# The mixer gates of a decoder layer as seven block products by tokens, ahead of all branch projections

## The chip, the cores and the metric

The kernel runs on one core of one Trainium2 chip. The metric is the device time of one execution in microseconds (us). Three runs of the kernel before gave 1073.43, 1072.18 and 1070.83 us, so the median is 1072.18 us.

The engines are named as in the profile: PE (TensorE, matrix products), PEld (its weight loads), DVE (VectorE), ACT (ScalarE), POOL (GpSimd) and SP (SyncE, here only a queue that issues transfers). A matmul has a moving operand, 512 or 256 columns wide here, and a stationary operand of 128 x 128, which PEld loads.

## The reference

One layer of a hybrid decoder on x of 512 tokens by 1024 features, in fp32. What matters here:

```python
proj = x @ w_in                       # q, k, v of three mixers, and gates: 3 x 1024 columns
o_da, o_sb, o_dl = ...                # three causal attentions, each 512 tokens x 512 features
g = sigmoid(gates).reshape(B, S, 3, D)
merged = g[0] * (o_da @ w_branch_da) + g[1] * (o_sb @ w_branch_sb) + g[2] * (o_dl @ w_branch_dil)
x = layer_norm(alpha * x + merged @ w_out)                       # LayerNorm 1
c = square(relu(x @ w_up)) @ w_down
ple = sigmoid(x @ w_ple_gate) * (p @ w_ple)
x = layer_norm(alpha * x + c + ple)                              # LayerNorm 2
```

## The kernel before

Precision. Every large fp32 product is made of three products in fp32r. Both factors are split into a high part and a rest, and h·h, h·l and l·h are added up in one PSUM bank. So each block of a product costs three matmuls. Weights arrive in **chunks** of 128 x 1024 fp32 (512 KB). A chunk is loaded by SP into one of 4 raw buffers (`fill`, `raw`, L207). ACT then casts it to the high part (`wh`, L235) and DVE subtracts to get the rest (`wl`, L238). There are 7 buffers for split chunks (`RING`), so splitting runs up to 7 chunks ahead of the matmuls that use them.

Items. The program is a list of **items**. One item is a run of matmuls into one PSUM bank (`mm`) and what takes the result out of it (`ev`). The loop at the end of `trunk` writes the items out one after the other. It issues the evacuation of the item before, splits one or two chunks (`pump`), adds up some weights (`add`), and calls `step`, which moves each attention head that is under way on by one piece. A head is a generator: its logits, its softmax and its value product are separate pieces. An item that yields in the middle of its matmuls gets a second `step` there. From this list a planner makes a fixed order for each engine, normally that of the list, but it places work that is ready ahead of work that it expects to be waiting.

Buffers. PSUM has 8 banks: 2 `mm` banks, which the items use in turn, and 6 `at` banks for the heads, for transposes and for sums that stay open over several items. SBUF has 48 general slots of 128 x 512 fp32 (`slot`) and two buffers of 8 x 512 columns with the tags XH and XL, which hold x transposed (`xhT`, `xlT`) and later LayerNorm 1's output transposed (`x1hT`, `x1lT`).

The order of items. Item 0 and the 58 after it project q, k, v (`t_item`: weights stationary, x moving, the result transposed, 24 matmuls; `v_items`: x stationary, weights moving, the result by tokens, 24 matmuls). Then come the **gates**: 24 `t_item`s, one per gate and 128 columns, each evacuated to a slot `graw`. Six come ahead of the first branch item. The rest alternate with the **branch items** (L401 to L427): for each of 8 column tiles three items of 12 matmuls, then the sigmoid (L394), a multiplication (L416), an addition (L420), and a split of the merged column tile into `mh` and `ml` (L425, L426). The sb and dil heads have to be done before item 65, the da heads before item 70. `wout_items` (L519 to L521) multiply the merged tiles, stationary, by w_out. LayerNorm 1 follows per 128 tokens (`ln1_gen`): four transposes per half (L567), splits into XH and XL (L551, L552). The next product, the input gate of the embedding (`wg_items`), and the MLP are already done by **seven products** of half-sized blocks in place of eight (Strassen's scheme in Winograd's form). It needs sums of weight blocks and of operand blocks.

Weight sums. `totals` queues the sums of weight blocks. Each set of four blocks takes four copies from DRAM to DRAM on SP (L174) and four accumulating transfers on POOL (L176). Each of the latter also waits for a recent cast of ACT, so that they keep pace. `add` issues the next one of the list, from item 24 on in the kernel before.

Of the kernel before, what the change touches and what calls it, by code (L numbers as in the profile page):

```python
# [9 lines left out]
F32 = mybir.dt.float32  # L10
# [7 lines left out]
P = 128  # L18
# [16 lines left out]
def main_order():  # L35
# [14 lines left out]
    for j in range(8):  # L50
        for i in range(3):
            o += [("T", "gate", 8 * i + j)]
# [3 lines left out]
def trunk(tc, a, out):  # L56
    nc = tc.nc
    es = ExitStack()
    with es:
# [209 lines left out]
        gate_raw = {}  # L269
# [16 lines left out]
        def t_evac(name, j):  # L286
            def ev(ps):
# [5 lines left out]
                elif name == "gate":  # L293
                    t = slot("graw")
                    cp(t, ps)
                    gate_raw[j] = t
# [75 lines left out]
        for kind, name, j in order[2:]:  # L372
            if kind == "T":
                if name == "gate":
                    continue
# [10 lines left out]
        sg = {}  # L386

        last_exp = [None]

        def gate_sig(i, j):  # L390
            t = gate_raw.pop(8 * i + j)

            with tc.issue_after(last_exp[0]):
                nc.scalar.activation(t, t, AF.Sigmoid)  # L394
            sg[i, j] = t

        def branch_items(j, between=()):
            c1 = chunk(a["wb1"][j].rearrange("p k m -> p (k m)"), 1024)
            c2 = chunk(a["wb2"][j].rearrange("p k m -> p (k m)"), 512)
            for n, i in enumerate((1, 2, 0)):  # L400
                if n == 2:  # L401
                    for t in between:
                        t_item(*t)
                    if j == 0:
                        first_da.append(len(items))
                def mm(ps, i=i):
                    c = c2 if i == 2 else c1
                    for k in range(4):
                        s = slice(((i % 2) * 4 + k) * P, ((i % 2) * 4 + k) * P + P)
                        h, lo = oTs[4 * i + k]  # L410
                        mm3(ps, c["h"][:, s], c["l"][:, s], h, lo, k == 0, k == 3)

                def ev(ps, i=i, n=n):
                    gate_sig(i, j)
                    g = sg.pop((i, j))
                    nc.vector.tensor_mul(g, g, ps)  # L416
                    if n == 0:
                        merged[j] = g
                    else:
                        nc.vector.tensor_add(merged[j], merged[j], g)  # L420
                    if n == 2:
                        m = merged[j]
                        h = slot("mh", F32R)
                        lo = slot("ml", F32R)
# [1199 lines left out]
```

## Time and profile before

| | |
|---|---|
| median of three runs | 1072.18 us (1070.83 to 1073.43) |
| the profiled execution, its own time | 1073.58 us |
| its span, first to last instruction | 1071.8 us |
| granted PE clock over the span | 0.998 |
| busy: PE, PEld, DVE, ACT, POOL | 1056.0, 907.8, 719.9, 528.3, 83.0 us |
| moved by DMA | 203.87 MB, mean 190 GB/s |

How to read it: a matmul's row has a modelled end, so matmuls overlap in the rows. What counts is the distance from one start to the next. Rows of the view by windows have the stretch, its length, then per engine the busy time and in brackets the number of instructions, then the granted PE clock, the share of time in which the DMA engines were busy, and GB/s. Rows of the view by time have start, duration, engine, line, operation, output<-inputs, shapes and count; in square brackets stands how long the engine had been idle and what ended that. Rows of the view by lines end with busy time, mean duration in ns, and idle time before.

### The profile page before, as it was taken

How to read it: one execution, taken by the hardware profiler on the slowest of the kernel's cores; microseconds unless marked ns; L12 is line 12 of the kernel's file. 1: busy time of each engine (PE TensorE's matmuls, PEld its weight loads, DVE VectorE, ACT ScalarE, POOL GpSimd, SP SyncE). 2: the span in 40 equal slices, each digit the busy share in tenths (PEclk: the TensorE clock that was granted, in tenths of full speed). 3: DMA queues.
4: the chain of work that ended last, by engine and by line, in shares of the span. 5: the costliest groups of instructions: out<-in, count | busy, mean ns of one | idle time of the engine just before them, and what ended most of it. 6: DMA issues, size and time to landing. Idle time of an engine off the chain costs nothing. (4 is left out here: it accounts for less than half of the span.)

```text
span 1071.8 us, 14697 instructions
## 1 busy us (share of the span) xinstructions
PE 1056.0 (99%) x5543; PEld 907.8 (85%) x5543; DVE 719.9 (67%) x1264; ACT 528.3 (49%) x866; POOL 83.0 (8%) x106
## 2 busy tenths in 40 slices
PE   8999999999999999999999999999999999999996
PEld 6888788999888888888888888888989989989985
DVE  5988577656443756655444445898786787787786
ACT  5665445435232545545333333375666567557551
POOL 0000200010011101011101110100100010000000
PEclk9999999999999999999999999999999999999999
DMA  7643545393777647575798757349989895655722
GB/s 275 189 175 123 174 166 134 122 255 98 236 217 199 192 139 209 172 204 163 202 259 226 189 160 243 110 132 279 245 215 258 253 257 194 196 177 178 236 79 79
DMA packets 61624, 203.87 MB, mean 190 GB/s; under 512 B 7387, under 2 KB 8299, under 8 KB 60465
## 3 DMA queue, kind: packets, MB, share of 16 engines
q1 hardware_dynamic: 41536, 164.03, 43.9%
q0 software_dynamic: 19440, 37.98, 20.5%
q8 instruction: 43, 0.70, 0.3%
q10 hardware_dynamic: 576, 0.92, 0.2%
q14 instruction: 29, 0.23, 0.1%
HBM read 200.78 MB, written 73.42 MB: 256 GB/s over the span
## 5 line engine op out<-in xcount | busy, mean ns | idle before, releaser
L235 ACT CAST wh<-raw 128x1024 fp32r<-128x1024 f32 (+1 forms) x231 | 238.9, 1036 | 296.6 <-PE mm L88 159.5
L238 DVE TENSOR_TENSOR wl<-raw,wh 128x1024 fp32r<-128x1024 f32 (+1 forms) x231 | 277.2, 1205 | 141.0 <-ACT wh L235 137.1
L87 PE MATMUL mm<-xhT,wh 128*128 128x512 f32 x496 | 196.4, 396 | 0.0
L89 PE MATMUL mm<-xhT,wl 128*128 128x512 f32 x496 | 194.2, 392 | 0.0
L88 PE MATMUL mm<-xlT,wh 128*128 128x512 f32 x496 | 194.0, 391 | 0.0
L89 PEld LDWEIGHTS mm<-xhT,wl 128*128 128x128 f32 x496 | 93.2, 188 | 19.6
L87 PEld LDWEIGHTS mm<-xhT,wh 128*128 128x128 f32 x496 | 93.3, 188 | 19.3 <-issue 1.1
L88 PEld LDWEIGHTS mm<-xlT,wh 128*128 128x128 f32 x496 | 93.3, 188 | 17.9
L744 PE MATMUL mm<-x1hT,wh 128*128 128x256 f32 x256 | 72.5, 283 | 2.4 <-DVE cut L756 2.4
L746 PE MATMUL mm<-x1hT,wl 128*128 128x256 f32 x256 | 72.5, 283 | 0.0
L745 PE MATMUL mm<-x1lT,wh 128*128 128x256 f32 x256 | 72.5, 283 | 0.0
L348 PE MATMUL mm<-wh,xhT 128*128 128x512 f32 x160 | 64.8, 405 | 0.0
L350 PE MATMUL mm<-wh,xlT 128*128 128x512 f32 x160 | 63.2, 395 | 0.0
L349 PE MATMUL mm<-wl,xhT 128*128 128x512 f32 x160 | 63.0, 394 | 0.0
L744 PE MATMUL mm<-xs,wh 128*128 128x256 f32 x192 | 54.5, 284 | 0.0
L745 PE MATMUL mm<-xs,wh 128*128 128x256 f32 x192 | 54.4, 283 | 0.0
L746 PE MATMUL mm<-xs,wl 128*128 128x256 f32 x192 | 54.3, 283 | 0.0
L176 POOL DMA_DIRECT2D total<-total x34 | 30.2, 954 | 278.7 <-ACT wh L235 233.1
L744 PEld LDWEIGHTS mm<-x1hT,wh 128*128 128x128 f32 x256 | 49.1, 192 | 2.8 <-issue 2.6
L745 PEld LDWEIGHTS mm<-x1lT,wh 128*128 128x128 f32 x256 | 49.1, 192 | 0.3
L746 PEld LDWEIGHTS mm<-x1hT,wl 128*128 128x128 f32 x256 | 49.2, 192 | 0.0
L350 PEld LDWEIGHTS mm<-wh,xlT 128*128 128x128 f32 x160 | 37.9, 237 | 3.9
(388 smaller groups left out, 2187.1 us busy)
## 6 DMA issues: line engine op xcount, KB each, us to landing
raw<-total SPq DMA_DIRECT2D x68, 512.0 KB, 4.3
raw<-in_wt_dram SPq DMA_DIRECT2D x62, 512.0 KB, 4.8
total<-total POOLq DMA_DIRECT2D x34, 512.0 KB, 9.5
total<-in_wu_dram SPq DMA_DIRECT2D x32, 512.0 KB, 6.8
total<-in_wd_dram SPq DMA_DIRECT2D x28, 512.0 KB, 6.6
raw<-in_wd_dram SPq DMA_DIRECT2D x25, 512.0 KB, 4.5
raw<-in_wu_dram SPq DMA_DIRECT2D x24, 512.0 KB, 4.6
raw<-in_wv_dram SPq DMA_DIRECT2D x20, 512.0 KB, 4.5
```

Of the source, the lines that this page charges most:

```text
L87: nc.tensor.matmul(ps, wh, xh, start=start, stop=False, skip_group_check=True)
L88: nc.tensor.matmul(ps, wh, xl, start=False, stop=False, skip_group_check=True)
L89: nc.tensor.matmul(ps, wl, xh, start=False, stop=stop, skip_group_check=True)
L176: i = nc.gpsimd.dma_start(t, s, accum_op=OP.add, max_dma_last_dim=2048)
L235: i = nc.vector.tensor_copy(h, raw) if c.get("dve") else nc.scalar.copy(h, raw)
L238: i = nc.vector.tensor_sub(lo, raw, h.bitcast(F32))
L348: nc.tensor.matmul(ps, x1, c["h"][:, s], start=k == 0, stop=False)
L349: nc.tensor.matmul(ps, x1, c["l"][:, s], start=False, stop=False)
L350: nc.tensor.matmul(ps, x2, c["h"][:, s], start=False, stop=k == 7)
L744: nc.tensor.matmul(o, c["h"][:, s], h, start=first, stop=False, skip_group_check=True)
L745: nc.tensor.matmul(o, c["h"][:, s], lo, start=False, stop=False, skip_group_check=True)
L746: nc.tensor.matmul(o, c["l"][:, s], h, start=False, stop=last, skip_group_check=True)
```

## The change

The gates leave `t_item`. For each of the three gates (in the order 1, 2, 0) `seven` makes 14 items of 12 matmuls: seven products of a 256-token block of x by a 512 x 512 block of weights, each for two tiles of 128 tokens. x is stationary now, the weights move, and the result is by tokens. All 42 stand ahead of all branch items (items 59 to 100). Six more sets of weight sums are queued, ahead of all others, and `add` begins at item 7 with other rates. The operand sums of x are made from x loaded again (`x_load`, `x_sum`).

The branch items become 8 per branch by tokens: oT is stationary, the weights move. Branch 0 (da) is first, then 2, then 1, the last by rows. Heads of sb and dil leave oT whole, and `halves` splits it ahead of the branch. The merged tiles, now by tokens, are turned on PE (`turn`, 32 transposes) into XH and XL, which `wout_items` then read. `wout_items` get a second step. LayerNorm 1's transposed output takes XH and XL after that. `seven` also replaces `wg_items`, with the same products, order and banks.

```diff
-    for j in range(8):
-        for i in range(3):
-            o += [("T", "gate", 8 * i + j)]
...
+        def seven(ws, ops, fin, two):
...
+                def bank():
+                    if p == 1 or two and p == 5:
+                        chain["XY"[p == 5], r] = at_bank()
+                    if p in (1, 6, 7, 4):
+                        return chain["X", r]
+                    if two and p in (5, 3):
+                        return chain["Y", r]
+                    return mm_bank()
...
+                    for k in range(4):
+                        c = cs[k // 2]
+                        s = slice((k % 2) * 512, (k % 2) * 512 + 512)
+                        h, lo = operand(ops, p, k, q)
+                        nc.tensor.matmul(ps, h, c["h"][:, s], start=k == 0 and begins, stop=False,
+                                         skip_group_check=True)
+                        nc.tensor.matmul(ps, h, c["l"][:, s], start=False, stop=False, skip_group_check=True)
+                        nc.tensor.matmul(ps, lo, c["h"][:, s], start=False, stop=k == 3 and ends,
+                                         skip_group_check=True)
+
+                def ev(ps):
+                    if p in (1, 5, 6):
+                        t = slot("cut")
+                        nc.scalar.copy(t, ps)
+                        cut[p, r] = t
+                        if p == 6 and not two:
+                            nc.vector.tensor_sub(t, cut[5, r], t)
+                    elif p == 2:
+                        t = cut.pop((1, r))
+                        nc.vector.tensor_add(t, t, ps)
+                        fin(r, 0, t)
+                    elif p == 7:
+                        t = cut.pop((5, r))
+                        nc.vector.tensor_sub(t, t, ps)
+                        fin(r + 2, 1, t)
+                    elif p == 3:
+                        t = cut.pop((6, r))
+                        if two:
+                            nc.vector.tensor_sub(t, ps, t)
+                        else:
+                            nc.vector.tensor_add(t, ps, t)
+                        fin(r, 1, t)
+                    else:
+                        fin(r + 2, 0, ps)
+                item(cs if r else [], mm, ev, need=cs, bank=bank, size=2)
...
+        def x_load(kp):
+            for p, k, t in ((1, 2 * kp, B0), (5, 2 * kp, B1), (2, 2 * kp + 4, B0), (4, 2 * kp + 4, B1)):
+                b = slot("xq").rearrange("p (k t) -> p k t", k=2)
+                nc.sync.dma_start(b, xt[:, k:k + 2, t])
+                xq[kp, p] = b
+
+        def x_sum(p, kp):
...
+            nc.vector.tensor_tensor(src, i, j, op=o)
+            nc.scalar.copy(h, src)
+            nc.vector.tensor_sub(lo, src, h.bitcast(F32))
...
+        gate_w = [block_weights("wga", i) for i in GATES]
+        wg_w = block_weights("wg")
+        gates_at = len(items)
+        for n, i in enumerate(GATES):
+            seven(gate_w[n], x_ops, gate_fin(i), False)(1, 2, 5, 6, 7, 3, 4)
+        for kp in range(2):
+            hook(gates_at - 2 + kp, lambda kp=kp: x_load(kp))
+            for n, p in enumerate((5, 6, 7, 3)):
+                hook(gates_at + 2 * n + kp, lambda kp=kp, p=p: x_sum(p, kp))
...
+                def ev(ps, tt=tt, half=half, key=key):
+                    g = gate_t.pop(key)
                     nc.vector.tensor_mul(g, g, ps)
...
+                    if (tt, half) not in merged:
+                        merged[tt, half] = g
+                        return
+                    nc.vector.tensor_add(merged[tt, half], merged[tt, half], g)
+                    if by_row and half:
+                        pending.append(turn(tt))
+                item(need if tt == 3 else [], mm, ev, need=need, size=2)
+
+        first_branch = len(items)
+        branch(0, False)
+        branch(2, False)
+        branch(1, True)
...
+        def turn(tt):
+
+            yield
+            if not mT:
+                mT.extend(one.tile([P, 8, 512], F32R, name=nm(n), tag=n, bufs=1) for n in ("XH", "XL"))
+            q = slice(tt * P, tt * P + P)
+            for half in range(2):
+                tp = at_bank()
+                for b in range(4):
+                    nc.tensor.transpose(tp[:, b * P:b * P + P], merged[tt, half][:, b * P:b * P + P], ident)
+                t3 = tp.rearrange("p (k t) -> p k t", k=4)
+                h, lo = [b[:, 4 * half:4 * half + 4, q] for b in mT]
+                nc.scalar.copy(h, t3)
+                nc.vector.tensor_sub(lo, t3, h.bitcast(F32))
+            yield
...
-            if n >= 24 and not wout_at + 2 <= n < wout_at + 16:
+            if n >= 7 and not wout_at + 4 <= n < wout_at + 22:
                 due[0] += it["size"]
-                while due[0] >= 3:
-                    due[0] -= 3
+                rate = 2.3 if n < gates_at else 4.5 if n < first_branch else 3
+                while due[0] >= rate:
+                    due[0] -= rate
                     add()
```

More of the change, by code (lines that the diff above doesn't have):

```diff
@@ L385, in trunk @@
         merged = {}
[L386 to L407, printed above, removed]
+        at = {}
@@ L428, in branch_items @@
[L428 to L446 removed]
+                        nc.tensor.matmul(ps, h[:, q], c["h"][:, s], start=k == 0, stop=False)
@@ L505, in load_xn @@
                 xn[tt, h] = t
[L507 removed]
+        mT = []
         def wout_items():
```

305 lines of the change are left out of this document (141 added, 164 removed).

## The prediction, on record before the result

> **What bounds the kernel now.** I read the windows of 50 us first, then the groups by line, then the view by time where PE had been idle.
>
> ```profile
> PE 1056.0 (99%) x5543; PEld 907.8 (85%) x5543; DVE 719.9 (67%) x1264; ACT 528.3 (49%) x866; POOL 83.0 (8%) x106
> ```
> ```profile
> 500.00:550.00 50.00, 50.00 (x224) 41.17 (x223) 23.38 (x29) 16.62 (x22) 7.26 (x8) 1.00 0.86 224
> 700.00:750.00 50.00, 49.17 (x242) 41.16 (x242) 45.09 (x65) 31.53 (x51) 3.56 (x4) 1.00 0.72 205
> 750.00:800.00 50.00, 47.62 (x345) 45.16 (x345) 39.97 (x50) 34.00 (x48) 6.17 (x7) 1.00 0.85 230
> 800.00:850.00 50.00, 50.00 (x320) 45.57 (x319) 37.66 (x44) 29.56 (x39) 4.40 (x5) 1.00 0.94 261
> 1050.00:1071.80 21.80, 13.36 (x71) 11.37 (x69) 14.30 (x33) 3.27 (x8) 2.06 (x3) 0.92 0.20 73
> ```
> ```profile
> 559.74 0.39 PE L87 MATMUL mm<-oTh,wh 128*128 128x512 f32 x1
> ...
> 563.82 0.39 PE L87 MATMUL mm<-oTh,wh 128*128 128x512 f32 x1
> ```
>
> PE sets the time from end to end. Its 15.8 us of idle time (1071.8 - 1056.0) lie mostly at the two ends, 8.4 of them in the last window (21.80 - 13.36). Inside, only 700 to 800 loses 0.83 and 2.38 us, where DVE is busy for 45.09 and 39.97 of 50. Busy time says little about the pace, because the rows of matmuls overlap. The pace is the distance between starts: 18 steps from 559.74 to 563.82, so **0.2267 us for a matmul of 512 columns**, under a row of 0.39. A matmul taken away is worth 0.2267 us as long as the next one is ready. The granted clock is 1.00 in these windows, so nothing is to be won or lost there.
>
> **The matmuls that go.** Gates before: 24 items of 24, so 576. After: 3 gates x 7 products x 2 token tiles x 12, so 504. The 72 fewer are worth 72 x 0.2267 = **-16.3 us**. Orientation changes (x stationary), but one LDWEIGHTS per matmul stays. The branches keep 288 matmuls and w_out 192.
>
> **The transposes that come.** 32 of them turn the merged tiles. LayerNorm 1 does eight of the same kind in one go:
>
> ```profile
> 683.95 0.39 PE L521 MATMUL mm<-wh,ml 128*128 128x512 f32 x1
> 683.96 1.02 PEld L567 LDWEIGHTS at<-ident,xn 128*128 128x128 f32 x8
> 684.38 0.69 DVE L525 SCALAR_TENSOR_TENSOR xn<-xn,mm 128x512 f32<-128x512 f32 x1 [0.95 <-PE mm L521]
> 684.82 1.08 ACT L551 CAST x1hT<-at 128x512 fp32r<-128x512 f32 x2 [15.70 <-PE at L567]
> 685.72 0.68 DVE L552 TENSOR_TENSOR x1lT<-at,x1hT 128x512 fp32r<-128x512 f32 x1
> ```
>
> 1.02 / 8 = 0.128 us each, so 32 cost **+4.1 us**. They lie on PE and nothing hides them. (The Trainium skill, TensorE: Matmul & The Clock Gate, Part 4: PE-mode transpose, puts a transpose in a kernel at about 275 ns. Its estimate would be 8.8 us and would halve the gain after the next terms. The trace's row of one transpose is as long, but its pace is under half of that, so the trace decides.)
>
> **XH and XL are taken.** Before, LayerNorm 1's first transposed tile is written while w_out's last item runs (684.82, above). After, the merged tiles sit in XH and XL until w_out's last matmul has read them, so that split comes late. What is late next is product 1 of the embedding's gate. From the rows: DVE takes a finished bank 0.43 us after its last matmul starts (683.95 to 684.38), the cast is 1.08 / 2 = 0.54, the rest 0.68. The next matmul starts some 0.07 + 0.43 + 0.54 = 1.04 us after the last in place of 0.23, so 0.8 lost. The third needs the low part at 1.04 + 0.68 = 1.72 and would be due at 1.04 + 2 x 0.23 = 1.50: 0.2 more. **+1.1 us** with hand-overs, if ACT and DVE are free then. Bounds: 0, if the planner finds PE other work, and 4, if two weight splits stand ahead on both engines.
>
> **DVE in the first gate.** A product item uses a chunk per 12 matmuls, so weight splits come twice as often, just where the da heads still run. Counting the code's steps (two per item that yields, one per product item), the last six of the 16 da blocks begin in the gates, and their last piece falls into item 80. So what is left of them lies on gate 1 and a third of gate 2. What they need is in before's window from da_k's last evacuation to the end of the heads:
>
> ```profile
> 437.00:507.00 70.00, 70.00 (x353) 58.62 (x351) 40.60 (x94) 37.36 (x85) 8.59 (x9) 1.00 0.62 172
> ```
> ```profile
> L238 DVE TENSOR_TENSOR wl<-raw,wh 128x1024 fp32r<-128x1024 f32 (+1 forms) x11 | 12.4, 1127 | 9.2 <-ACT wh L235 6.3 <-PE at L1278 2.8
> L98 DVE COPY graw<-mm 128x512 f32<-128x512 f32 x5 | 3.5, 692 | 5.1 <-PE mm L89 5.1
> L416 DVE TENSOR_TENSOR graw<-graw,mm 128x512 f32<-128x512 f32 x2 | 1.4, 688 | 2.3 <-PE mm L89 2.1 <-ACT graw L394 0.3
> L420 DVE TENSOR_TENSOR graw<-graw,graw 128x512 f32<-128x512 f32 x1 | 0.7, 693 | 0.0
> ```
> ```profile
> L87 PE MATMUL mm<-xhT,wh 128*128 128x512 f32 x72 | 28.9, 402 | 0.0
> L88 PE MATMUL mm<-xlT,wh 128*128 128x512 f32 x72 | 28.3, 392 | 0.0
> L89 PE MATMUL mm<-xhT,wl 128*128 128x512 f32 x72 | 28.2, 391 | 0.0
> L87 PE MATMUL mm<-oTh,wh 128*128 128x512 f32 x13 | 5.1, 404 | 0.0
> L88 PE MATMUL mm<-oTl,wh 128*128 128x512 f32 x12 | 4.8, 400 | 0.0
> L89 PE MATMUL mm<-oTh,wl 128*128 128x512 f32 x11 | 4.3, 392 | 0.0
> ```
> ```profile
> L238 DVE TENSOR_TENSOR wl<-raw,wh 128x1024 fp32r<-128x1024 f32 (+1 forms) x231 | 277.2, 1205 | 141.0 <-ACT wh L235 137.1
> ```
>
> The heads take 40.6 - 12.4 - 3.5 - 1.4 - 0.7 = 22.6 us of DVE, and of PE 70.0 - 252 x 0.2267 = 12.9. Gate 1 adds on DVE 14 splits of 1.205 (16.9), `x_sum` with 8 x 2 passes of 0.69 (11.0) and 8 evacuating passes (5.5): 56 us with the heads. PE has 168 x 0.2267 + 12.9 = 51. So DVE is over full in gate 1 by some 5 us at most. Over items 59 to 80 it has 26.5 + 11.0 + 8.3 + 22.6 = 68.4 against PE's 59.8 + 12.9 = 72.7, 94%. What it is late with can slide: splits run 7 chunks ahead, and the heads have until item 101. I take **+2 us** (bounds 0 and 5), by the windows at 700 and 750, which lose 0.8 and 2.4 at 90 and 80%. ACT (37.36 of 70 there) has room for its own share.
>
> **The rest.** Gates 2 and 3 need 1.205 + 8/14 x 0.69 = 1.6 us of DVE per item of 2.72, which PE covers. The branches have on DVE 24 multiplications, 16 additions, 8 rests from `turn` and 16 passes of `halves` at up to 0.69 (44 us) and some 16 splits (19): 63 of PE's 69 us. **+0.5** (0 to 2). The passes for `graw` that go (24 evacuations, ACT and DVE in turn, and 8 splits into `mh`, `ml`) were hidden under PE, so they earn nothing. Earlier sums move DRAM copies and loads on SP and POOL:
>
> ```profile
> L1043 POOL DMA_DIRECT2D sh<-rv x8: 692/754/910, 123.0 to 304.9; - x8
> L1053 DVE COPY shf<-sh x8: 418/421/453, 167.6 to 340.1; 128x512 f32<-128x512 f32 x8
> ```
> ```profile
> total<-total POOLq DMA_DIRECT2D x34, 512.0 KB, 9.5
> xn<-in_xn_dram SPq DMA_DIRECT2D x8, 256.0 KB, 9.3
> ```
> ```profile
> ACT wh L235 <- PE mm L88: 159.5, 59, 4.7
> ```
>
> Bias tables queue on POOL, now behind some 12 accumulating transfers. The first is issued at 123.0 and DVE turns it at 167.6, so they may come 30 us late before DVE, and the heads behind it, wait; a chain of three transfers of 9.5 us fits. `x_load` puts 8 loads on SP two items ahead of `x_sum`: 2 x 5.4 us plus heads, against 9.3 to land. If that cover is gone, DVE waits a few us with 7 split chunks ahead of PE: ACT waited 59 times for PE to free a buffer, so the ring is full as a rule. A chunk per 2.72 us and 0.16 sums per us in the gates is less than in 800 to 850, where PE was busy for 50.00 with DMA at 0.94. I book 0, with 3 us on the high side.
>
> **Sum.** -16.3 + 4.1 + 1.1 + 2.0 + 0.5 = -8.6. The profiled execution has a span of 1071.8 and 1.8 around it, so 1073.58 becomes 1065.0. It stands 1.4 above the median of the runs, so the median becomes 1072.18 - 8.6 = **1063.6**.
>
> **Rivals.** *No stall counts.* The planner fills the gaps: -16.3 + 4.1 = -12.2, so 1060.0. For it: PE at 50.00 in nearly every window. Against it: 700 to 800.
>
> *The bounds add up, still a gain.* 5 in gate 1, 4 at XH, 2 in the branches, so -16.3 + 4.1 + 11 = -1.2, which with half of that is 1065 to 1071; I put it at 1068.5.
>
> *DVE paces the evacuations: slower.* Products 2 and 5 both use the two `mm` banks, so the matmuls of product 5 wait until DVE has added up product 2's result, behind whatever DVE has ahead of that.
>
> ```profile
> L744 PE MATMUL mm<-x1hT,wh 128*128 128x256 f32 x256 | 72.5, 283 | 2.4 <-DVE cut L756 2.4
> ```
> ```profile
> 754.99 0.35 PE L744 MATMUL mm<-x1hT,wh 128*128 128x256 f32 x1 [2.38 <-DVE cut L756]
> ```
> ```profile
> 691.74 1.07 ACT L551 CAST x1hT<-at 128x512 fp32r<-128x512 f32 x2
> 692.13 0.68 DVE L525 SCALAR_TENSOR_TENSOR xn<-xn,mm 128x512 f32<-128x512 f32 x1
> 692.73 2.35 DVE L238 TENSOR_TENSOR wl<-raw,wh 128x1024 fp32r<-128x1024 f32 x2
> 695.00 1.28 DVE L552 TENSOR_TENSOR x1lT<-at,x1hT 128x512 fp32r<-128x512 f32 x2
> ```
>
> Exactly this wait, on a sum of products 1 and 2, held PE for 2.38 us, once in the 256 matmuls of its group. The last fence shows how: the cast was there at 692.3, and DVE came to its rest only at 695.00, after two weight splits. (The Trainium skill, TensorE: Matmul & The Clock Gate, Part 2, calls VectorE's queue strictly first in, first out, and the trace agrees here with 2.7 us.) Two token tiles in three gates make 6 such waits: 6 x 2.38 = 14.3, against -12.2 + 1.1, so 1072.18 + 3.2 = 1075.4. It decides from 11.1 / 6 = 1.85 us per wait. Against it: the MLP has the same pair of products eight times over and waited once, and an item of 2.72 us lies between the banks' uses.
>
> *The sums aren't there.* POOL falls behind, and a gate's load waits for its sum. By item 59 the rate has issued 90 of them, and the gates need 48: under 3 in 100, some 1080.
>
> **Chances.** Forecast (1061.5 to 1067) 0.45; no stall 0.20; bounds add up 0.17, of which 0.03 ends above 1070; DVE paces 0.13; sums or another late transfer 0.05. What a measurement here can tell from no change is about 0.2%, 2.1 us. So faster (under 1070.0) is 0.45 + 0.20 + 0.14, less 0.02 for a tail of the forecast, = 0.77. The same is 0.03 + 0.02, and 0.03 and 0.01 from the milder half of the last two rivals, = 0.09. Slower is the 0.10 and 0.04 left of these, = 0.14. The range reaches from 1058.5, the no-stall case with 1.5 us of the old idle time gone too, to 1075.5, the far rival.
>
> **What would show it.** Right: `seven`'s matmuls in the gates start 0.227 us apart; the 32 transposes cost 4 us; PE idles 1 us once, ahead of the first product after w_out; PE's busy time falls by about 12. Wrong: PE waits for DVE at the start of products 5 in every gate, windows in the gates or branches under 48 of 50, a wait for `total` or `xq` ahead of PE, or a wider step between the gates' matmuls.

## The result, and the profile after

The changed kernel takes **1087.96 us** (median of four runs, 1087.08 to 1089.89) against 1071.99 us of the kernel before. The ratio is 1.0151, with a 95% interval of 1.0132 to 1.0170: 1.5% slower, where 1063.6 us was predicted. The profiled execution took 1088.46 us, with a span of 1086.8 us and a mean granted clock of 0.991.

The first part of its page shows that PE has fewer matmuls, as planned (5503 in place of 5543), and idles for 34.6 us in place of 15.8. Its busy time falls by 3.8 us and not by the 12 that the prediction gave as a sign, in part because PE ran at half its clock for some 10 us (below), which makes its rows longer:

```profile
PE 1052.2 (97%) x5503; PEld 899.4 (83%) x5503; DVE 753.3 (69%) x1306; ACT 559.1 (51%) x906; POOL 105.3 (10%) x130
```

The view by windows, first of the kernel before (stretch, length, busy time of PE, PEld, DVE, ACT and POOL, clock, DMA share, GB/s), then of the changed kernel:

```profile
100.00:150.00 50.00, 50.00 (x232) 38.75 (x232) 34.37 (x58) 23.00 (x38) 7.40 (x12) 1.00 0.48 153
...
900.00:950.00 50.00, 50.00 (x320) 45.64 (x319) 38.46 (x48) 32.59 (x44) 0.00 (x0) 1.00 0.60 187
```
```profile
100.00:150.00 50.00, 45.41 (x189) 33.19 (x188) 27.08 (x47) 18.40 (x32) 13.85 (x19) 0.90 0.62 175
...
400.00:450.00 50.00, 48.20 (x246) 40.59 (x245) 30.92 (x71) 23.59 (x57) 4.60 (x5) 1.00 0.64 190
450.00:500.00 50.00, 48.23 (x245) 39.52 (x244) 45.48 (x109) 42.83 (x88) 6.84 (x6) 1.00 0.76 221
500.00:550.00 50.00, 50.00 (x230) 41.55 (x229) 30.29 (x35) 34.83 (x48) 4.58 (x5) 1.00 0.82 246
550.00:600.00 50.00, 50.00 (x222) 41.39 (x222) 32.94 (x41) 24.89 (x33) 4.48 (x5) 1.00 0.86 265
...
900.00:950.00 50.00, 43.60 (x267) 38.90 (x266) 33.57 (x41) 25.01 (x35) 4.41 (x5) 0.97 0.86 278
950.00:1000.00 50.00, 46.41 (x298) 41.56 (x297) 36.11 (x43) 31.19 (x42) 2.64 (x3) 1.00 0.88 260
```

Three places lose time: 100 to 150, 400 to 500, and the MLP at 900 to 1000. The gates' first stretch, 450 to 500, loses 1.8 us, and the rest of the gates and branches (500 to 650) nothing. How far behind the changed kernel is at each point is read from the same event in both. The last projection of da_k is evacuated at 438.20 before and 449.82 after (view by time, before, then after), so 11.6 us are lost by then. The last result of w_out comes at 692.13 (in the prediction) and 692.28. So **gates, branches and w_out gained 11.5 us**, and all of it went to pay for the first 450.

```profile
438.20 0.58 ACT L125 ACTIVATE da_ka<-mm 64x512 fp32r<-64x512 f32 x1
```
```profile
449.82 0.59 ACT L122 ACTIVATE da_ka<-mm 64x512 fp32r<-64x512 f32 x1
...
692.28 0.68 DVE L647 SCALAR_TENSOR_TENSOR xn<-xn,mm 128x512 f32<-128x512 f32 x1
```

The MLP's first product starts 1.1 us later than before (744.9 against 743.8), and the end comes 15.0 later. So 13.9 us are lost in the MLP.

**The table loads at 105 us.** The view of one tile (`oh`, the one-hot table from which the bias tables are made), before and after. Each row has count, duration in ns, first and last start:

```profile
L1031 PE MATMUL at<-oh,rel x10: 269/376/589, 110.7 to 119.4; 33*4 33x256 f32 x4, 33*4 33x512 f32 x2, 33*4 33x128 f32 x2, 33*4 33x384 f32 x2
L1064 POOL DMA_DIRECT2D oh<-in_onehot_dram x1: 754/754/754, 99.7 to 99.7; - x1
...
DMA to landing us min/median/max: 2.8/2.9/3.4
```
```profile
L1142 POOL DMA_DIRECT2D oh<-in_onehot_dram x1: 1367/1367/1367, 104.5 to 104.5; - x1
...
DMA to landing us min/median/max: 9.4/9.6/10.0
```

Before, POOL issued the loads at 99.7, the first landed at 103.1, and PE used it at 110.7: 7.6 us to spare. After, they stand behind seven accumulates in POOL's order, start 4.8 us later and land 6.6 us slower, at 114.5. PE's next matmul in order reads `oh` and starts at 114.64. The view puts its wait down to "issue", that is, to nothing that the profile shows, but the landing comes just ahead of the start, and the run named early bears it out. Then PE's clock is halved (view by time, then windows of 5 us, after):

```profile
114.64 2.29 PE L1109 MATMUL at<-oh,rel 33*4 33x512 f32 x4 [4.58 <-issue]
```
```profile
110.00:115.00 5.00, 0.41 (x2) 0.11 (x2) 1.23 (x1) 0.02 (x1) 0.93 (x1) 0.94 1.02 249
115.00:120.00 5.00, 5.00 (x13) 2.25 (x12) 1.29 (x3) 3.02 (x7) 1.17 (x2) 0.50 0.95 272
120.00:125.00 5.00, 5.00 (x12) 3.28 (x11) 2.12 (x5) 1.78 (x4) 0.51 (x1) 0.54 0.02 4
```

A gap of 4.6 us and 10 us at 0.50 to 0.54 of the clock make the loss of some 9 (4.6, and by estimate half of the 10). At 430 us a smaller loss follows: a power step (`ms`) on POOL also stands behind accumulates, DVE waits 3.19 us for it and PE 1.61 us for DVE.

**The MLP.** PE waits for weights (view by time, after, PE's rows and ACT's):

```profile
911.57 2.00 ACT L232 CAST wh<-raw 128x1024 fp32r<-128x1024 f32 x2
916.67 1.05 ACT L232 CAST wh<-raw 128x1024 fp32r<-128x1024 f32 x1 [3.10 <-DMA raw<-in_wu_dram]
922.55 0.50 PE L910 MATMUL at<-wl,hh 128*128 128x512 f32 x1 [1.24 <-DVE wl L235]
929.55 0.39 PE L824 MATMUL mm<-XH,wl 128*128 128x256 f32 x1 [1.68 <-DVE wl L235]
932.49 0.58 ACT L829 COPY cut<-mm 128x512 f32<-128x512 f32 x1 [14.77 <-PE mm L824]
932.97 0.62 ACT L796 CAST hh<-hs 128x512 fp32r<-128x512 f32 x1
933.49 3.88 ACT L232 CAST wh<-raw 128x1024 fp32r<-128x1024 f32 x4
934.59 0.39 PE L822 MATMUL mm<-XH,wh 128*128 128x256 f32 x1 [2.14 <-ACT wh L232]
```

ACT stood for 14.77 us at a copy of a product that PE had yet to make, and four weight casts stood behind it. In the kernel before (view by time) such a copy comes behind the casts and waits for nothing:

```profile
923.83 1.05 ACT L235 CAST wh<-raw 128x1024 fp32r<-128x1024 f32 x1 [0.31 <-PE mm L833]
926.59 1.05 ACT L235 CAST wh<-raw 128x1024 fp32r<-128x1024 f32 x1 [1.70 <-PE mm L745]
927.54 0.58 ACT L751 COPY cut<-mm 128x512 f32<-128x512 f32 x1
```

### The profile page after: what moved, and what is told of

Read it like the earlier page. It is cut to its first block, busy times and chain, and to the rows that moved or that the text cites. A ratio compares the mean times of both kernels' runs of the same rounds, so it can differ in the third digit from the quotient of the medians.

```text
span 1086.8 us, 14845 instructions
## 1 busy us (share of the span) xinstructions
PE 1052.2 (97%) x5503; PEld 899.4 (83%) x5503; DVE 753.3 (69%) x1306; ACT 559.1 (51%) x906; POOL 105.3 (10%) x130
## 4 chain that ended last, share of the span: by engine, by line
PE 79%; DMA 7%; DVE 6%; issue 5%; ACT 3%; POOL 0%; SPq 0%; DVEq 0%; ACTq 0%; POOLq 0%
PE mm L85 5%; PE mm L84 5%; PE mm L86 5%; PE mm L822 4%; PE mm L824 4%; PE mm L823 4%; PE mm L340 3%; PE mm L342 3%; PE mm L341 3%; PE at L430 3%; PE at L428 3%; PE at L431 3%; DMA raw<-total 2%; DVE wl L235 2%; PE mm L548 2%
## 5 line engine op out<-in xcount | busy, mean ns | idle before, releaser
L235 DVE TENSOR_TENSOR wl<-raw,wh 128x1024 fp32r<-128x1024 f32 x245 | 297.2, 1221 | 130.0 <-ACT wh L232 128.0
L232 ACT CAST wh<-raw 128x1024 fp32r<-128x1024 f32 x245 | 256.0, 1050 | 235.8 <-PE mm L85 61.2
L84 PE MATMUL mm<-xhT,wh 128*128 128x512 f32 x304 | 121.0, 398 | 0.0
L86 PE MATMUL mm<-xhT,wl 128*128 128x512 f32 x304 | 120.0, 395 | 0.0
L85 PE MATMUL mm<-xlT,wh 128*128 128x512 f32 x304 | 119.9, 394 | 0.0
L822 PE MATMUL mm<-XH,wh 128*128 128x256 f32 x256 | 73.2, 286 | 4.0 <-ACT wh L232 2.1
L824 PE MATMUL mm<-XH,wl 128*128 128x256 f32 x256 | 73.3, 286 | 2.4 <-DVE wl L235 2.4
L823 PE MATMUL mm<-XL,wh 128*128 128x256 f32 x256 | 73.0, 285 | 0.0
L84 PEld LDWEIGHTS mm<-xhT,wh 128*128 128x128 f32 x304 | 57.6, 189 | 11.4 <-PE mm L86 0.4
L822 PEld LDWEIGHTS mm<-XH,wh 128*128 128x128 f32 x256 | 49.7, 194 | 4.8 <-ACT wh L232 2.3
L824 PEld LDWEIGHTS mm<-XH,wl 128*128 128x128 f32 x256 | 49.7, 194 | 2.8 <-DVE wl L235 2.8
```

The source lines that it names most:

```text
L84: nc.tensor.matmul(ps, wh, xh, start=start, stop=False, skip_group_check=True)
L85: nc.tensor.matmul(ps, wh, xl, start=False, stop=False, skip_group_check=True)
L86: nc.tensor.matmul(ps, wl, xh, start=False, stop=stop, skip_group_check=True)
L232: i = nc.vector.tensor_copy(h, raw) if c.get("dve") else nc.scalar.copy(h, raw)
L235: i = nc.vector.tensor_sub(lo, raw, h.bitcast(F32))
L822: nc.tensor.matmul(o, c["h"][:, s], h, start=first, stop=False, skip_group_check=True)
```

## The experiments

Theory A: the products and turned rows gain what was forecast, and the 48 further weight sums cost all the rest. Theory B: the gates' own work costs it. More theories came with the findings.

**nosums: the change without the gates' sums.**

```diff
-        gate_w = [block_weights("wga", i) for i in GATES]
+        gate_w = [{p: [a["wga"][i][p % 4, c].rearrange("p k n -> p (k n)") for c in range(2)]
+                   for p in range(1, 8)} for i in GATES]
...
-            if n >= 7 and not wout_at + 4 <= n < wout_at + 22:
+            if n >= 24 and not wout_at + 2 <= n < wout_at + 16:
...
-                rate = 2.3 if n < gates_at else 4.5 if n < first_branch else 3
+                rate = 3
```

> The changed kernel without the gates' 48 weight sums: the gates' seven products read the unsummed weight blocks in the sums' places (so the gates' values are not the reference's; every product, load of a block and element operation stays), and the other sums start at item 24 at one per three size units with the pause as before. Theory A (the products and the turned rows gain what the traces show, about 11 us, and all that was lost comes from the sums): 1060 to 1066 us. Theory B (the loss is in the gates' own element operations, slots and loads, and would come without sums too): 1076 to 1088 us. The first use of the one-hot table should come without a gap on TensorE and the MLP without waits for weights by A; by B the MLP's waits stay.

Measured: 1068.34 us, ratio 0.9973 (0.9954 to 0.9993). The gap at 114 us and the waits in the MLP are gone, which speaks for A, but the time is 2 us above its range (ten runs, 1066.28 to 1075.41). PE lost 5 us at 615 us, where ACT waited for a load (view by time, then by windows):

```profile
619.33 0.62 ACT L1203 CAST pTh<-pT 128x512 fp32r<-128x512 f32 x1 [9.91 <-DMA pT<-in_pT_dram]
```
```profile
600.00:650.00 50.00, 44.86 (x205) 36.78 (x204) 30.86 (x44) 11.83 (x16) 2.37 (x3) 0.93 0.73 233
```

The cast of the embedding's input stands ahead of the casts that turn the merged rows. So one more load, late among many, holds all that ACT has behind it in its order.

**sums_only: the kernel before, with 48 more sums and nothing else.**

```diff
+            for _ in range(3):
+                totals([[a["wg"][i, c].rearrange("p k n -> p (k n)") for i in range(4)] for c in range(2)])
...
-            if n >= 24 and not wout_at + 2 <= n < wout_at + 16:
+            if n >= 7 and not wout_at + 4 <= n < wout_at + 22:
                 due[0] += it["size"]
-                while due[0] >= 3:
-                    due[0] -= 3
+                rate = 2.3 if n < 59 else 4.15 if n < wout_at else 3
+                while due[0] >= rate:
+                    due[0] -= rate
```

> The kernel before with nothing changed but the sums: 48 more sums of weight blocks ahead of the others (blocks of the embedding gate are added up three times into rows that nobody reads), at the changed kernel's rates from item 7 on and with its longer pause. Theory A (the sums alone cost 9 us at 105 to 125 us, 2 to 3 us at 430 us and some 14 us in the MLP): 1088 to 1098 us. Theory B (the sums cost little, the gates' other work is the loss): 1072 to 1077 us.

Measured: 1089.09 us, ratio 1.0152 (1.0137 to 1.0167), the whole loss of the change without any of its products, and within A's range. By 448 us it is 9.6 behind. Its late loss lies elsewhere than A had it: the MLP is clean, and w_out waits for the residual's load (view by time, then by windows).

```profile
669.49 0.69 DVE L525 SCALAR_TENSOR_TENSOR xn<-xn,mm 128x512 f32<-128x512 f32 x1 [10.48 <-DMA xn<-in_xn_dram]
```
```profile
650.00:700.00 50.00, 46.47 (x203) 38.12 (x202) 27.71 (x42) 8.29 (x10) 4.42 (x5) 0.97 0.80 244
```

That its size equals the change's loss is partly chance, since the change gains 11 elsewhere and loses more.

**early: the table loads ahead of the sums.** `load_oh` issues the three loads that `tables` issued.

```diff
+            if n == 6:
+                load_oh()
             if n == 13:
                 pending.append(tables())
```

> The changed kernel with the three one-hot table loads issued on POOL at item 6, ahead of the first accumulate, instead of at item 13 behind seven. Theory A (TensorE's 4.6 us gap at 114 us is the table load's place in POOL's queue, and the half clock of the 10 us after it follows from the gap): 1079 us (1077 to 1081), the granted clock of 110 to 125 us back at 1.00. Theory C (the gap is the DMA engines' fullness, which the load meets wherever it stands, or the time is given back at the next wait): 1084 to 1089 us.

Measured: 1078.06 us, 9.9 less than the change, ratio 1.0051 (1.0034 to 1.0069). Theory A holds and C falls: the gap is gone, although the DMA engines are just as full in that stretch (windows of 5 us):

```profile
110.00:115.00 5.00, 5.00 (x23) 3.26 (x21) 2.27 (x3) 4.49 (x8) 1.95 (x3) 1.00 1.04 238
115.00:120.00 5.00, 5.00 (x21) 3.16 (x21) 2.65 (x5) 1.67 (x3) 0.50 (x1) 1.00 0.86 261
```

**rate2: more sums in gates and branches, fewer late.**

```diff
-                rate = 2.3 if n < gates_at else 4.5 if n < first_branch else 3
+                rate = 2.3 if n < gates_at else 2.3 if n < first_branch else 2
```

> The changed kernel with more sums in the gates and branches (one per 2.3 size units in the gates instead of 4.5, one per 2 in the branches instead of 3), so that 24 fewer are left for after w_out. Theory A (the MLP's 14 us are sums and copies that run beside its own weight loads): 1074 to 1080 us. Theory D (there is no room earlier either: the gates' and branches' loads, at a DMA share of 0.82 to 0.86 now, are held up instead): 1086 to 1095 us.

Measured: 1102.50 us, ratio 1.0285: a miss for A, and above D's range too. DMA is at 1.03 in 550 to 600, and the loss moves to w_out and to 800 to 850 us (PE busy 41.06 of 50, clock 0.90).

**late0: early, without the 48 last sums.**

```diff
-                w = totals(q)
+                w = totals(q) if b < 5 else [{p: x[p % 4] for p in range(1, 8)} for x in q]
```

> The changed kernel with the table loads at item 6 (as in the run named early), and without the 48 sums of the MLP's weight blocks 5 to 7: the products of those blocks read unsummed blocks, so the output is not the reference's, while every load of a block, product and element operation stays and as many sums run as in the kernel before. Theory A (the waits of 900 to 990 us are raw loads held up by copies and accumulates beside them): 1066 to 1071 us, landing of the raw loads at 900 to 980 us back at 4 to 5 us, TensorE busy 50 of 50 us there. Theory B (the MLP is slower through slots, the order of casts or the longer queue of elements): 1076 to 1080 us.

Measured: 1064.18 us, ratio 0.9920 (0.9901 to 0.9938), 13.9 less than early and 2 us below A's range. The MLP is whole again (windows):

```profile
900.00:950.00 50.00, 50.00 (x301) 44.87 (x300) 40.66 (x50) 29.78 (x38) 0.00 (x0) 1.00 0.59 185
950.00:1000.00 50.00, 50.00 (x326) 45.89 (x325) 38.01 (x46) 29.34 (x39) 0.00 (x0) 1.00 0.61 192
```

So the last sums make the MLP's loss. By their bytes, or by what they do to the order?

**raw5, spread, nosums_pt: three misses of A.** More buffers for loads:

```diff
-        NSLOT = 48
+        NSLOT = 46
...
-        RING, RAW = 7, 4
+        RING, RAW = 7, 5
```

> The run named early with five raw buffers instead of four, paid for by two of the 48 shared slots (46). With four buffers and one chunk of weights used up in 12 matmuls (2.72 us) a landing of 9 to 10 us is just what the ring can bear; with five it is 13.6 us. Theory A (the MLP's waits come as soon as the landing exceeds what the ring covers): 1068 to 1075 us. Theory E (the DMA engines move no more, however many loads are under way; each lands later by as much): 1077 to 1080 us, landings of 11 to 12 us.

Measured: 1080.60 us, no gain; raw loads at 895 to 945 us land in 3.4 to 12.1 us. The windows shift the loss: against early PE wins 2.3 us at 900 to 950 (46.21 of 50) and loses 3.7 at 400 to 450 (43.99). Two slots fewer came with the fifth buffer, so the run doesn't show what more buffers alone do. Sums drawn forward:

```diff
-                rate = 2.3 if n < gates_at else 4.5 if n < first_branch else 3
+                rate = 2.3 if n < 22 else 1.4 if n < 47 else 4 if n < gates_at else 6 if n < first_branch else 3
...
-            if n == wout_at + 2:
+            if n == wout_at + 5:
                 load_pT()
```

Spread also has the pause of the kernel before, and early's edit, as raw5 and all that follow have, except nosums_pt and tie_only.

> All sums and products of the changed kernel, with the table loads at item 6, the sums drawn forward into the projections, where a chunk is used up only every 5.4 us (one per 1.4 size units in items 22 to 46, 4 to the gates, 6 in the gates, 3 after that), the pause of the kernel before, and the load of the embedding's input three items later. Theory A (the loss is where the sums stand and not how many there are): 1060 to 1070 us. Theory D (there is no room for 48 more sums anywhere): 1076 to 1095 us, with a gap of 4 to 5 us and half clock behind it in the projections instead.

Measured: 1092.68 us, ratio 1.0183. The MLP is nearly clean, but 350 to 500 us loses 22. The longest wait of PE there is 11.23 us, behind casts of ACT that wait for raw loads. These land in 7.6 to 10.2 us while the DMA share is 1.02 to 1.15 (windows of 5 us, 430 to 445). Another 4.6 us go to `x_sum`, which holds DVE until the gates' token loads are there (view by time, PE's row, then DVE's):

```profile
442.54 0.58 PE L135 MATMUL at<-da_ka,da_qa 128*128 128x256 f32 x1 [11.23 <-ACT da_ka L126]
...
451.46 0.69 DVE L500 TENSOR_TENSOR xq<-xq,xq 128x512 f32<-128x512 f32 x1 [5.11 <-DMA xq<-in_xT_dram]
```

The same move of `load_pT` in nosums:

> The run named nosums (gates without sums, their products on unsummed blocks) with the load of the embedding's input three items later, so that its cast, which landed 14.1 us after its issue and held ScalarE for 9.9 us, stands behind the merged rows' casts. Theory A (that one wait took nosums from 1060 us to 1068 us, and the products and turned rows gain 11 us): 1059 to 1063 us. Theory B (the branches and the turned rows cost more than was thought, whatever ScalarE waits for): 1066 to 1070 us.

Measured: 1067.95 us (ten runs, 1066.26 to 1075.99), in B's range. The planner put the cast where it had been. In the profiled execution, the longest of the ten, PE still waited 3.1 us there, and 4.8 us behind the `xq` loads. So it doesn't tell A from B, and the 1060 us that A gives without these waits were not reached.

**moved, best1, best2: loads moved, a hole in the sums.**

```diff
-            hook(gates_at - 2 + kp, lambda kp=kp: x_load(kp))
+            hook(gates_at - 6 + 2 * kp, lambda kp=kp: x_load(kp))
...
+            if n == wout_at - 16:
+                read_pT()
+            if n == wout_at - 12:
                 ln_consts("ln1_g", "ln1_b")
-                for tt in range(4):
-                    load_xn(tt)
+            if wout_at - 8 <= n < wout_at and (n - wout_at) % 2 == 0:
+                load_xn((n - wout_at + 8) // 2)
```

`read_pT` loads what `load_pT` then casts. Best1 adds to moved (best2 has 1.6, 4 and 2 for 1.3, 5 and 2.5):

```diff
-                rate = 2.3 if n < gates_at else 4.5 if n < first_branch else 3
+                rate = 2 if n < 22 else 1.3 if n < 45 else 5 if n < first_branch else 2.5 if n < wout_at else 3
...
-            if n >= 7 and not wout_at + 4 <= n < wout_at + 22:
+            if n >= 7 and not 45 <= n < gates_at + 4 and not wout_at + 2 <= n < wout_at + 16:
```

> The run named early with three more groups of loads moved ahead and nothing else: the gates' eight token loads four items and two items earlier (items 6 and 4 before the gates instead of 2 and 1), the embedding's input read 18 items before its cast, and the norm's rows and the residual's eight loads drawn out over 12 items instead of one burst 6 items before w_out. Sums as in the changed kernel. Theory A (each wait of 3 to 6 us near 430 and 620 us was one of these loads at the head of VectorE's or ScalarE's order; the MLP's late sums stay): 1072 to 1077 us, the MLP's waits of 900 to 990 us unchanged. Theory D (full DMA engines make some load late wherever it is put): 1078 to 1085 us.

> The run named moved with the sums drawn forward and a hole in them: one per 2 size units up to item 21, per 1.3 up to item 44, none from there to the fourth item of the gates (where the attention's small steps on POOL and the token loads stand), per 5 in the gates, per 2.5 in the branches, and the pause of the kernel before. Theory A (in the run named spread the projections up to 350 us and the MLP bore their sums, and only 380 to 470 us didn't): 1062 to 1070 us. Theory D: 1076 to 1095 us, with new waits where the sums now stand.

> The same hole with fewer sums ahead of it: one per 1.6 size units in items 22 to 44, per 4 in the gates, per 2 in the branches. Theory A: 1064 to 1072 us. Theory D: 1076 to 1095 us; if the branches can't hold one per 2 (as the run that raised the rates there suggests), the waits come at 600 to 700 us.

Measured: 1081.17, 1082.95 and 1093.79 us, all beyond A's ranges and within D's. Best1 has a clean MLP (PE 49.58 of 50 at 900 to 950) and loses at 300 to 450. Best2 loses 10 us at 900 to 950 alone. They move the same bytes as early does, so the volume doesn't set the time by itself.

**thin: the late sums with an eighth of the bytes.**

```diff
+            t, s = t[:rows, :], s[:rows, :]
...
-                w = totals(q)
+                w = totals(q, P if b < 5 else 16)
+                if b >= 5:
+                    w = [{p: x[p % 4] for p in range(1, 8)} for x in q]
```

> The run named early, all its 92 copies and 92 accumulates in their places in SyncE's and POOL's order, but the last 48 sums (the MLP's weight blocks 5 to 7) work on 16 of 128 rows, an eighth of the bytes, and the products of these blocks read unsummed blocks as in the run named late0, so the output is not the reference's. It lies between early (1078 us, full bytes) and late0 (1064 us, no such sums). Theory F (the MLP's waits come from the bytes that the copies and accumulates move beside the raw loads): 1063 to 1068 us, DMA share of 900 to 1000 us near 0.65. Theory G (they come from the places of the copies and accumulates in the two queues and the waits between them, whatever they move): 1074 to 1080 us.

Measured: 1076.52 us, 1.5 less than early, in G's range. Theory F falls: DMA at 900 to 950 is at 0.47, less than before the change, and PE waits for the same weights, to the hundredth as long as in the changed kernel (windows, then view by time):

```profile
900.00:950.00 50.00, 44.19 (x265) 39.41 (x264) 32.46 (x41) 24.76 (x35) 3.84 (x5) 0.97 0.47 151
```
```profile
912.14 0.50 PE L913 MATMUL at<-wl,hh 128*128 128x512 f32 x1 [1.24 <-DVE wl L236]
...
919.15 0.39 PE L827 MATMUL mm<-XH,wl 128*128 128x256 f32 x1 [1.68 <-DVE wl L236]
...
922.09 0.58 ACT L832 COPY cut<-mm 128x512 f32<-128x512 f32 x1 [17.99 <-PE mm L827]
...
924.19 0.39 PE L825 MATMUL mm<-XH,wh 128*128 128x256 f32 x1 [2.14 <-ACT wh L233]
```

So these waits don't go by the bytes, and the fixed order of the engines is the next suspect. The number of weight casts that stand ahead of the first `cut` copy of each of the MLP's last blocks, in ACT's order as built, fits that (the rows of the traces give the same counts to within three). 14 casts lie between blocks when the order is regular:

| kernel | casts ahead of the copy | PE busy of 50 at 800, 850, 900, 950 |
|---|---|---|
| late0 | 169, 183, 197, 211, 225 | 50.00, 50.00, 50.00, 50.00 |
| changed, early, thin | 169, 182, 192, 204, 222 | 50.00, 49.84, 43.60, 46.41 (changed) |
| rate2 | 162, 183, 197, 211, 225 | 41.06, 50.00, 50.00, 50.00 |
| best2 | 169, 181, 193, 206, 225 | 50.00, 45.04, 40.05, 46.60 |

Where a copy slips four or more casts forward, PE loses time in that block or the next. That is a match and not yet a test.

**tied, tie_only, tied_da: ACT's order restored.**

```diff
                         t = slot("cut")
-                        nc.scalar.copy(t, ps)
+                        with tc.issue_after(st["cast"]):
+                            nc.scalar.copy(t, ps)
```

> The run named early with all its sums in full, and one constraint more: in the MLP each ScalarE copy of a product into a cut tile is issued behind the newest weight cast, as the kernel's text has them (written order), instead of up to seven casts ahead of it (192, 204 and 222 casts ahead of three of these copies in early; 197, 211 and 225 in late0 and here). Bytes, queues and places of the sums stay. Theory H (the MLP's 14 us are the planned order on ScalarE: a copy that waits for its product with the next products' casts behind it): 1063 to 1069 us. Theory F (bytes): 1076 to 1080 us, waits for weights at 900 to 990 us as before.

> The changed kernel with the constraint on ScalarE's copies alone; the one-hot table loads stay behind the accumulates. Theory H: 1072 to 1078 us (1088 less 11 to 14 us in the MLP, the 9 to 10 us at 110 to 125 us stay). Theory F: 1086 to 1090 us.

Measured: 1077.09 us (ratio 1.0049) and 1089.14 us (1.0159): no gain, though ACT's numbers are late0's. Both times lie where theory F had them, and H as put falls. The copy now waits behind casts whose raw loads are late: in tied ACT's casts wait up to 6.60 us for a load at 900 to 930. SP's loads wait up to 9.2 us for the low halves (`wl`) that free the raw buffers, and DVE's additions (`xn`) still stand ahead of these. Tied_da adds, in the sums' rates:

```diff
-                rate = 2.3 if n < gates_at else 4.5 if n < first_branch else 3
+                rate = 1.85 if n < 46 else 4.5 if n < first_branch else 3
...
-            if n >= 7 and not wout_at + 4 <= n < wout_at + 22:
+            if n >= 7 and not 46 <= n < gates_at and not wout_at + 4 <= n < wout_at + 22:
```

> The run named tied with the sums of items 46 to 58 (the differential attention's small steps on POOL) drawn ahead of them, one per 1.85 size units from item 7. Theory: the 2 to 3 us wait near 420 us for POOL's small power step, which stands behind accumulates, goes or halves, and nothing else moves: 1061 to 1068 us; if the DMA engines have no room ahead of item 46: 1070 us or more.

Measured: 1068.93 us, ratio 0.9975 (0.9961 to 0.9988), 0.9 us above its theory's range. The wait for POOL's power step falls from 2.4 to 0.6 us, as expected. But 6 us more went than that, in the MLP, which was not expected: 900 to 950 is at 50.00 (43.48 in tied) and only 950 to 1000 still loses 4.7, with as many sums and bytes as in tied. DVE's rows offer a reason. A block of the MLP ends in eight additions. Between the first and the last of those that begin at 895 to 909 us, DVE makes 6 low halves in tied_da, as in late0 and in the kernel before, and 3 in the changed kernel, early, thin and tied. PE is busy for 50.00 of 50 at 900 to 950 in the first three, and for 43.48 to 44.19 in the other four. So other times of the sums gave another planned order on DVE, in a place where no sum had been taken away. This too is a match: the sums' times moved with the order.

**thin2, tied2, tied2_da: both orders restored.**

```diff
-                        nc.vector.tensor_add(t, t, ps)
+                        with tc.issue_after(st["low"]):
+                            nc.vector.tensor_add(t, t, ps)
```

> The run named thin (an eighth of the late sums' bytes, the products of those blocks on unsummed blocks, so not the reference's output) with two constraints on order: in the MLP ScalarE's copy of a product stands behind the newest weight cast, and VectorE's addition of a product behind the newest low half of a weight (162, 163, 164, 165 low halves ahead of the additions, one period as in late0; in early the order slips to 192 where late0 has 196 and to 202 where it has 208). Theory H (the planned order of ScalarE and VectorE makes thin's waits): 1062 to 1067 us, no wait over 1 us for weights at 900 to 990 us. Theory I (neither the bytes nor these orders): 1074 to 1078 us.

> The same two constraints on the run named early, sums in full. Theory H alone: 1063 to 1068 us. Theory HF (order and bytes each suffice: raw loads that land in 6 to 9 us beside full sums leave late weights even in the good order): 1074 to 1080 us, with the waits at ScalarE's and VectorE's operations that now stand behind late weights.

> The two constraints on the run named tied_da (1069 us; sums of items 46 to 58 drawn ahead), all sums in full. Theory H: 1062 to 1067 us. Theory HF: 1067 to 1072 us, as the one wait of 4.7 us that tied_da has left comes with late loads.

Measured: 1072.03, 1076.32 and **1067.05 us** (ratio of the last 0.9948, 0.9936 to 0.9961). With thin and early that makes four cases:

| us | full bytes | an eighth |
|---|---|---|
| planned order | 1078.06 (early) | 1076.52 (thin) |
| both orders tied | 1076.32 (tied2) | 1072.03 (thin2) |

Neither alone is worth 2 us, and so little is not clear of the scatter (the runs of early, thin and tied2 spread over 3.3 to 5.5 us each). Together they are worth 6.0 of the 13.9, which is clear of it. That this is more than the sum of both is not. HF is the nearest theory, but not the whole. Thin2 fell between the ranges of H and I, and in thin2 the constraint itself costs, as PE waits for the tied additions (groups of waits: us, times, longest; first tied2, then thin2):

```profile
PE mm L910 <- DVE xn L918: 5.3, 5, 1.9
```
```profile
PE mm L913 <- DVE xn L921: 3.3, 4, 1.2
```

How the other 8 us divide between that, other places in the order and the small transfers stays open. Full bytes alone don't make the loss, as tied2_da shows, at the edge between H's range and HF's, with every sum and product of the change (windows):

```profile
400.00:450.00 50.00, 49.55 (x251) 41.44 (x250) 40.06 (x95) 31.68 (x71) 3.65 (x4) 1.00 0.63 189
...
900.00:950.00 50.00, 49.78 (x298) 44.17 (x297) 39.01 (x48) 28.73 (x39) 3.51 (x4) 1.00 0.96 286
```

DMA is fuller than in the changed kernel (0.96 against 0.86), and PE waits for 0.2 us. This version is 1.9% faster than the change and 0.5% faster than the kernel before.

## Why the prediction was wrong, step by step

- **The products, transposes, DVE in gate 1, branches** (-16.3 + 4.1 + 2.0 + 0.5 = -9.7): right, and a little low. From da_k's end to w_out's end the change gained 11.5. The gates' matmuls start 0.227 us apart, as forecast: 22 steps in 5.00 us (view by time, after).

```profile
520.78 0.40 PE L431 MATMUL at<-wh,xs 128*128 128x512 f32 x1
...
525.78 0.39 PE L428 MATMUL at<-wh,xs 128*128 128x512 f32 x1
```

Eight transposes and the matmul behind them take 1.11 us from start to start at 635.48, so eight cost 0.88 and 32 some 3.5. Windows 500 to 600 are at 50.00, and 450 to 500 lost 1.8 with DVE at 45.48, as the +2.0 for gate 1 had it.
- **XH and XL** (+1.1): right. The MLP's first product comes 0.9 us later after w_out's last result than before (744.9 - 692.3 against 743.8 - 692.1). The first four steps from start to start in the embedding gate take 1.56 us (692.82 to 694.38) in place of 0.91; in the longest of them PE waits for the cast into XH.
- **Earlier sums, booked at 0**: this is the step that failed, by some 25 us: it put the price of 48 more sums at nothing. It held two claims and left out a third cost. *"so they may come 30 us late"* looked at the `sh` transfers and DVE. The first user of the table is PE, 7.6 us behind the landing, and the load came 11.4 late: +9 with the halved clock; early takes 9.9 off. *"A chunk per 2.72 us and 0.16 sums per us in the gates is less than in 800 to 850"* judged the gates by DMA share. That held for the gates, but the sums queued ahead push 48 others into the MLP, which the step didn't follow: +13.9, shown by late0; by which way the late sums do it is shown only in part. And nothing was said of the POOL step behind accumulates at 430, some 2 us, shown by tied_da.
- **The cover of `x_load`**, taken for enough: thin. It cost little here, but 4.8 us in one execution of nosums_pt and 4.6 in spread.
- **Rivals.** No stall and the added bounds both assumed the sums free. DVE pacing the evacuations fell: no product 5 waited in the gates. The late-sums rival (1080, 0.05) had the right cause and the wrong mechanism: no gate's load waited for its sum. Others' loads were late, and the order planned around the sums was another. (The words on VectorE's queue that the prediction takes from the Trainium skill stand in Part 1 of that page.)
- **The sum.** With the table early and the late sums out, late0 takes 1064.18 us, the predicted 1063.6 within its spread; the forecast was one of the core alone. That the total fits so well is partly luck. By the same events as above late0 is 2.7 us behind at da_k's end (440.93), gains 11.4 up to w_out's end (683.41) and nothing behind it, where 0, 9.7 and a loss of 1.1 were forecast. These three misses cancel.

## What to carry to other kernels

When work is moved ahead in a queue, follow what it pushes back, to the end of the program, and find the first user of every transfer behind it, on the engine that is the bound. DMA share alone is a poor judge: at 1.04 PE ran through in early, at 0.47 it stood in thin, and at 1.02 to 1.15 it stood in spread. When a planner lays out the order, compare the order of each engine as built, as added transfers can move a waiting copy ahead of the casts that feed the bound, here hundreds of microseconds away.

## What the runs showed of the hardware that was not expected

- A gap of 4.6 us on PE cost as much again: the granted clock was 0.50 and 0.54 in the 10 us behind it. Matmuls of 512 columns still start 0.43 us apart 9.8 us after the gap's end, in place of 0.23. In the first 6.2 of these PE had short matmuls of the bias tables and of attention. In nosums a gap of 4.84 us has transposes and matmuls of 512 columns behind it, and half pace ends after 4.4 us (view by time, nosums: the next start after that of 625.76 comes 0.26 later). That the short matmuls make the difference is not shown. (The Trainium skill, TensorE: Matmul & The Clock Gate, Part 1: The HAM clock gate, has half speed after an idle window of about 3.4 us and full speed after about as long of work. The first agrees. The way back took longer in both runs, 9.8 and 4.4 us.)

```profile
621.33 1.12 PE L663 MATMUL at<-ident,cut 128*128 128x128 f32 x4 [4.84 <-DVE cut L559]
...
625.76 0.42 PE L551 MATMUL mm<-wh,oTl 128*128 128x512 f32 x1
626.02 0.40 PE L549 MATMUL mm<-wh,oTh 128*128 128x512 f32 x1
```

- The same small load landed in 2.9 us in the kernel before, with no accumulate ahead of it, and in 9.6 us behind two of them. A cast's 512 KB load landed in 3.4 to 12.1 us among copies and accumulates (raw5).
- An eighth of the late sums' bytes left three waits of PE unchanged to 0.01 us (1.24, 1.68, 2.14).
